# Feed-forward down projections: high halves of the weights by a casting DMA, low halves by an ACT negation and a DMA that adds the weights

## The chip, the core and the metric

One core of one Trainium2 chip runs the whole program once. The metric is device time in microseconds, the median of the timed executions. TensorE (PE in the profile) multiplies, VectorE (DVE), ScalarE (ACT) and GpSimd (POOL) work element by element, SyncE (SP) issues DMAs. Each engine works through its own list of instructions in order and waits at semaphores for the others.

## What is computed

The reference is ten blocks in a row on one activation of 256 tokens by 1024 columns, all in float32. Six of them are the feed-forward block that the change touches:

```python
def swiglu(h, w_gate, w_up, w_down):
    return (jax.nn.silu(h @ w_gate) * (h @ w_up)) @ w_down
```

The inner width is 2816, so gate and up are 1024 x 2816 and down is 2816 x 1024. Each block has an RMS norm ahead of it, some one behind it, and a residual. Between the feed-forward blocks (F1, F3, F4, F6, F8, F10 in the code) stand a convolution with windowed attention ("even"), a forgetting attention ("fox"), an mLSTM ("ml") and a chunked attention with relative positions ("rel"). All weights are read once.

## The kernel before

**Two halves of each weight.** TensorE's fast float32 mode (fp32r) keeps fewer bits than float32. The kernel therefore splits every operand into a high half hi, rounded to fp32r, and a low half lo = w - hi, and makes each product from three matmuls: xh·wh + xh·wl + xl·wh (`mm3`). A matmul has 128 rows and 512 columns.

**Weight stream.** The weights come as 264 units of 1 MB, [128, 2048] each, in the order of use, through `unit` (lines 156 to 178). A DMA of SP loads a unit into one of two `raw` buffers (line 281). For each of the two halves of 1024 columns ACT casts raw to hi (line 207), and DVE forms lo = raw - hi (line 217). hi and lo lie in `hl`, a pool of 20 buffers of [128, 1024], four to a unit. An `hl` buffer is free again when the last matmul that reads it is done, a `raw` buffer when the last subtraction that reads it is done.

**A feed-forward block** (`ffn`) has 11 chunks of 256 inner columns. A chunk has three units: two of gate and up, one of down. For both token blocks b of 128 rows, 24 matmuls per block make gate and up in a PSUM bank (`mm`), ACT and DVE make silu(gate)·up from it, two transposes on PE (line 277) and a split on ACT and DVE give `gt`, and 12 matmuls per block add the chunk's part of the down projection into `acc`. So a chunk has 72 matmuls of 512 columns.

**Order.** Nothing is ordered by hand. The program records all operations with a priority each, and `schedule` plays them against a table of durations, one list per engine, picks buffers as they come free, and emits what results. The table `NUDGE` shifts the priorities of named pieces. The list of an engine is then fixed, and on the chip each instruction only waits for its data and buffers. `load(..., after=...)` adds an order in that plan alone; it makes no wait on the chip.

Of the kernel before, what the change touches and what calls it, by code (L numbers as in the profile page):

```python
# [15 lines left out]
       ("ACT", "PE"): 205.0}  # L16

# [50 lines left out]
class Op:  # L68
    __slots__ = ("eng", "dur", "em", "key", "n", "deps", "succ", "rd", "wr", "end", "start", "vs",
                 "lab", "table", "lat", "avail", "seq", "soft", "ins", "hist")  # L70


class Rec:
    def __init__(self, tc, tags, nudge):
        self.tc, self.nc = tc, tc.nc
        self.tags = tags
        self.ops = []
        self.key = 0.0
        self.grp = None
        self.lab = ""  # L80
        self.phys = {}
        self.nv = 0
        self.meas = None
        self.nudge = nudge
# [67 lines left out]
    def _add(self, o, key):  # L152
        o.key = self.key if key is None else key
        o.n = len(self.ops)
# [89 lines left out]
    def ttr(self, out, a, b, scale, init, op0, op1, accum, key=None):  # L244
        """out = (a op0 b) * scale, accum = its reduction by op1"""
        n = self.n_of(a)
        self.op("DVE", (66 + n) / 0.96 + 8, [a, b], [out, accum],
                lambda: self.nc.vector.tensor_tensor_reduce(  # L248
                    self.res(out), self.res(a), self.res(b), scale, init, op0, op1, self.res(accum)), key=key)
# [15 lines left out]
    def mm(self, out, l, r, start, stop, key=None):  # L265
        n = self.n_of(r)
        if r.v.dt == F32R:
            d = max(107.0 if self.shape(l)[1] > 64 else 53.5, n / 2.4) + 2.5
        else:
            ls = self.shape(l)  # L270
            d = 126.0 if ls[1] == 64 else 2 * max(107.0, n / 1.2) + 4
# [3 lines left out]
    def tr(self, out, in_, ident, key=None):  # L275
        self.op("PE", 109.0, [in_, ident], [out],
                lambda: self.nc.tensor.transpose(self.res(out), self.res(in_), self.res(ident)), key=key)  # L277
# [15 lines left out]
    def schedule(self, sem=130.0):  # L293
# [21 lines left out]
        engs = ["PE", "ACT", "DVE", "DMA"]  # L315
# [4 lines left out]
        table = None  # L320
# [7 lines left out]
        while left:  # L328
# [80 lines left out]
            d = o.dur  # L409
            if o.table is not None and table != o.table:  # L410
# [49 lines left out]
class Net:  # L460
# [40 lines left out]
    def near(self, key):  # L501
        return self.units.get(min(int(key), max(self.units, default=0)))

# [24 lines left out]

    def wsl(self, un, c0, n):
# [5 lines left out]
    def rstd(self, ss, w, n, key, more=False, cut=1):  # L535
        """[P, w] sums of squares (parts of them) -> rsqrt(ss / n + eps), Newton from the exponent trick"""
# [29 lines left out]
    def split_T(self, src, n, hi, lo, key, o0=0, pk=None):  # L566
        """transposes n [128,128] blocks of src into hi + lo at column block o0"""
# [10 lines left out]
    def ssq(self, b, key):  # L578
        """sums of squares of the halves of x"""
# [7 lines left out]
    def gain_T(self, b, g, key):  # L587
        """x * g, transposed and split"""
# [26 lines left out]
    def norm(self, b, g):  # L615
        """(x * g).T in two parts, and per token 1 / rms, half of it, half its square"""
# [9 lines left out]
    def mm3(self, out, x, w, first, last, key):  # L626
        """out += x.T @ w from halves: groups of one k-block"""
# [6 lines left out]
    def proj(self, b, xs, us, u0, n, per, grp=2):  # L634
        """bank [128, n] = x @ W; units hold `per` k-blocks of n columns each"""
# [16 lines left out]
    def oproj(self, b, acc, hi, lo, o0, un, u0, first, last):  # L652
        """acc[2 banks] += o @ W; unit holds 2 k-blocks of 1024 columns"""
# [13 lines left out]
    def postnorm(self, b, acc, g, scale):  # L667
        """x += scale * rmsnorm(acc) * g"""
# [22 lines left out]
    def ffn(self, gi, post, name, exps=lambda b, ch: False):  # L691
# [10 lines left out]
        for ch in range(NCH + 1):  # L702
            if ch < NCH:
                for i in range(3):
                    un[ch * 3 + i] = self.unit(u0 + ch * 3 + i)
# [36 lines left out]
    # the 4 heads of a group lie in the order HM: those on partitions 0-63 first, then those on 64-127  # L742
    def attn_group(self, b, key, qT, kT, v, bias, sgn, O, oc, den, sink=None, nd=2):
        """4 heads of one query block. qT [128, 2 pairs x 128]; kT, v: per pair or key block; sgn * (scores + bias) are negative logits"""
# [62 lines left out]
    def bias_tile(self, b, name, j, key):  # L807
        """additive bias of 4 heads of a query block: for one key block or two"""
# [14 lines left out]
    def k_T(self, b, kT, pt, key):  # L823
        """bank [128, 2 pairs x 128] -> kT [128, 2 pairs x 256]"""
# [4 lines left out]
    def qk_T(self, b, key, bank, rs, kT, sgn=1.0):  # L829
        """row-layout bank [tok, 512] -> (qT [128, nq*128] scaled, kT) via transposes"""  # L830
# [13 lines left out]
    def logsig(self, z, w, out, key):  # L844
        """out = min(z, 0) - log1p(exp(-|z|)), [P, w]"""
# [29 lines left out]
    def gates(self, b, xs, gu, u0, key):  # L875
        """bank [128, 16] = x @ W for 16 columns: W is the stationary side, the sum is turned afterwards"""
# [593 lines left out]
def _cols(w, c0, n):  # L1470
    """[1024, cols] -> units of n-wide columns, 2048 // n k-blocks each: [units, 128, 2048]"""
# [4 lines left out]
def _rows(w):  # L1476
    """[K, 1024] -> units of two k-blocks: [K / 256, 128, 2048]"""
# [11 lines left out]
def arrange(i):  # L1489
# [68 lines left out]
CFG = dict(lead=4, ahead=0, cb=2, fb=6, dd=4, ab=3, vb=2, ncst=784, stages=99, rk=3, bl=3, cg=6, vp=0, du=4, nd=0, k4=2, xb=1, k2=1)  # L1558

NUDGE = {  # L1560
# [17 lines left out]
    "even attn b1": -2, "even attn b1 p": -5, "even conv": -6, "even conv b0 p": 10.5, "even conv b1 p": 14,  # L1578
# [70 lines left out]
```

## Time and profile before

| | |
|---|---|
| median of 3 runs | 1593.97 us (1592.77 to 1594.99) |
| profiled execution, first to last instruction (span) | 1591.4 us |
| PE busy | 1573.6 us (99%) |
| DVE busy | 1015.5 us (64%) |
| ACT busy | 837.4 us (53%) |
| POOL busy | 0.2 us |
| DMA | 296.83 MB, queue of SP busy 50.9% of 16 engines |

The profiled execution lies 2.57 us under the median of the runs: its span counts from the first to the last instruction of the program, and what lies around it is in the timed runs alone. Matmuls are pipelined, and the ends of their rows are modelled, so PE's busy time also holds short waits between two matmuls.

### The profile page before, as it was taken

The numbers are of one execution on the slowest core, as the hardware profiler recorded it, in microseconds if no ns is written. First come the engines' busy times: TensorE is split into PE (matmuls) and PEld (weight loads), VectorE is DVE, ScalarE is ACT, GpSimd is POOL, SyncE is SP. The second block draws the span as 40 slices with busy tenths as digits, with TensorE's granted clock in tenths as the row PEclk, the third lists the DMA queues.
The fourth block names the chain that finished last, engine by engine and source line by source line (L and its number), as shares of the span: only waits on it lengthen the run. The fifth ranks groups of instructions, "written<-read, shape, count | busy, mean of one in ns | idle before, by whom it ended". The sixth has DMA issues, their size and how long they took to land.

```text
span 1591.4 us, 20430 instructions
## 1 busy us (share of the span) xinstructions
PE 1573.6 (99%) x7714; PEld 1289.5 (81%) x7714; DVE 1015.5 (64%) x1969; ACT 837.4 (53%) x1400; POOL 0.2 (0%) x4
## 2 busy tenths in 40 slices
PE   8999999999999999999999999999999999999998
PEld 6888888888888888887788888788888887788886
DVE  6555689854558555677964557887545576755544
ACT  6444556744455454566854445655444457754443
POOL 0000000000000000000000000000000000000000
PEclk9999999999999999999999999999999999999999
DMA  6655585355554555446444554445544645354542
GB/s 244 217 185 211 176 299 184 117 184 188 215 215 151 210 185 211 161 179 208 169 161 183 204 219 160 146 146 198 199 175 169 238 173 202 142 185 185 208 175 80
DMA packets 49587, 296.83 MB, mean 187 GB/s; under 512 B 5408, under 2 KB 8912, under 8 KB 16720
## 3 DMA queue, kind: packets, MB, share of 16 engines
q1 hardware_dynamic: 49488, 295.52, 50.9%
q8 instruction: 60, 0.98, 0.2%
q14 instruction: 39, 0.32, 0.1%
HBM read 294.43 MB, written 1.07 MB: 186 GB/s over the span
## 4 chain that ended last, share of the span: by engine, by line
PE 93%; DVE 3%; DMA 2%; ACT 1%; issue 0%; SPq 0%; ACTq 0%; DVEq 0%
PE mm L273 60%; PE acc L273 28%; PE mm L277 5%; DMA raw<-in_w 2%; DVE hl L217 1%; DVE b L236 1%; ACT hl L207 1%; ACT b L207 1%; DMA x<-in_x 0%; DVE s L236 0%; DVE xt L236 0%; DVE b L248 0%; ACT xt L207 0%; DVE x L236 0%; SPq L281 0%
## 5 line engine op out<-in xcount | busy, mean ns | idle before, releaser
L273 PE MATMUL mm<-hl,xt 128*128 128x512 f32 (+1 forms) x4224 | 1013.0, 393 | 0.6 <-DVE xt L217 0.3
L273 PEld LDWEIGHTS mm<-hl,xt 128*128 128x128 f32 x4224 | 778.0, 188 | 161.4 <-DVE hl L217 2.2
L217 DVE TENSOR_TENSOR hl<-raw,hl 128x1024 fp32r<-128x1024 f32 (+1 forms) x518 | 618.0, 1213 | 350.2 <-ACT hl L207 259.5
L207 ACT ACTIVATE hl<-raw 128x1024 fp32r<-128x1024 f32 (+1 forms) x518 | 522.3, 1048 | 332.6 <-DMA raw<-in_w 168.1
L273 PE MATMUL acc<-hl,gt 128*128 128x512 f32 x1584 | 385.8, 393 | 0.0
L273 PEld LDWEIGHTS acc<-hl,gt 128*128 128x128 f32 x1584 | 293.1, 188 | 59.4 <-ACT gt L207 0.2
L207 ACT ACTIVATE b<-mm,s 128x256 f32<-128x256 f32 (+2 forms) x188 | 94.0, 509 | 219.9 <-PE mm L273 214.7
L236 DVE SCALAR_TENSOR_TENSOR b<-mm,s,b 128x256 f32<-128x256 f32 x132 | 63.3, 481 | 98.4 <-ACT b L207 98.1
L277 PE MATMUL mm<-cst,b 128*128 128x128 f32 (+1 forms) x680 | 109.4, 272 | 3.0 <-DVE s L248 2.5
L277 PEld LDWEIGHTS mm<-cst,b 128*128 128x128 f32 (+1 forms) x680 | 85.4, 140 | 32.2 <-ACT b L207 3.7
L207 ACT ACTIVATE gt<-mm 128x256 fp32r<-128x256 f32 x132 | 50.0, 378 | 92.1 <-PE mm L277 84.6
L273 PE MATMUL acc<-hl,xt 128*128 128x512 f32 x384 | 96.0, 397 | 0.7 <-DVE xt L217 0.7
L217 DVE TENSOR_TENSOR gt<-mm,gt 128x256 fp32r<-128x256 f32 x132 | 55.2, 419 | 51.7 <-ACT gt L207 49.2
L273 PEld LDWEIGHTS acc<-hl,xt 128*128 128x128 f32 x384 | 70.0, 188 | 16.5 <-issue 1.4
L207 ACT ACTIVATE b<-b,s 128x128 f32<-128x128 f32 (+2 forms) x146 | 60.0, 442 | 15.0 <-DVE s L236 7.2
L236 DVE SCALAR_TENSOR_TENSOR s<-s 128x1 f32<-128x1 f32 (+2 forms) x260 | 47.8, 184 | 7.9
L207 ACT ACTIVATE b<-x 128x512 f32<-128x512 f32 x44 | 27.6, 628 | 23.0 <-DVE x L217 11.8
L207 ACT ACTIVATE xt<-mm 128x512 fp32r<-128x512 f32 x44 | 25.4, 595 | 22.0 <-PE mm L277 21.8
L236 DVE SCALAR_TENSOR_TENSOR b<-aT,cst,b 128x256 f32<-128x256 f32 x75 | 31.8, 477 | 0.0
L217 DVE TENSOR_TENSOR xt<-mm,xt 128x512 fp32r<-128x512 f32 x44 | 29.5, 685 | 3.0 <-ACT xt L207 2.4
L207 ACT ACTIVATE b<-mm 128x512 f32<-128x512 f32 (+4 forms) x44 | 21.5, 504 | 13.0 <-PE mm L277 11.2
L273 PE MATMUL mm<-aT,b 128*128 128x128 f32 (+1 forms) x232 | 28.2, 276 | 0.0
(75 smaller groups left out, 454.9 us busy)
## 6 DMA issues: line engine op xcount, KB each, us to landing
raw<-in_w SPq DMA_DIRECT2D x256, 1024.0 KB, 4.8
g<-in_gains SPq DMA_DIRECT2D x18, 512.0 KB, 6.2
b<-in_diag SPq DMA_DIRECT2D x8, 512.0 KB, 5.7
b<-dr SPq DMA_DIRECT2D x12, 256.0 KB, 5.3
g<-in_relb SPq DMA_DIRECT2D x4, 512.0 KB, 5.8
b<-in_diag SPq DMA_DIRECT2D x4, 448.0 KB, 5.3
x<-in_x SPq DMA_DIRECT2D x4, 256.0 KB, 5.3
raw<-in_w SPq DMA_DIRECT2D x4, 256.0 KB, 5.3
```

The source lines that it names most:

```text
L207: return self.nc.scalar.activation(self.res(out), self.res(in_), func, **kw)
L217: lambda: self.nc.vector.tensor_tensor(self.res(out), self.res(a), self.res(b), op), key=key)
L236: lambda: self.nc.vector.scalar_tensor_tensor(self.res(out), self.res(a), self.res(s), self.res(b), op0, op1, **kw), key=key)
L273: lambda: self.nc.tensor.matmul(self.res(out), self.res(l), self.res(r), start=start, stop=stop), key=key)
L277: lambda: self.nc.tensor.transpose(self.res(out), self.res(in_), self.res(ident)), key=key)
```

## The change

The down projection's units (one in three within the feed-forward blocks, 66 of 264) no longer go through `raw`. For each of their 132 halves, GpSimd issues a DMA that reads the float32 weights from memory and writes them into the hi buffer as fp32r, which casts on the way; ACT writes lo = -hi; and a second DMA of GpSimd reads the same weights again and adds them into lo. The other units are loaded and split as before. The cast on ACT is replaced one for one by the negation; 132 subtractions on DVE and 66 loads of 1 MB on SP go; 264 DMAs of 512 KB on GpSimd come in.

```diff
+    def pload(self, out, src, nbytes, key=None, add=False, after=None):
+        kw = dict(accum_op=ALU.add) if add else {}
+        o = self.op("POOL", 1100.0, [src] + [out] * add, [out],
+                    lambda: self.nc.gpsimd.dma_start(out=self.res(out), in_=self.res(src), **kw), lat=2000.0 + nbytes / 220.0, key=key)
+        if after is not None:
+            o.deps.append(after)
...
+    def unit_dma(self, u):
...
+        for c0 in range(0, 2048, 1024):
+            sl = slice(c0, c0 + 1024)
+            hi, lo = r.t("hl", name="hi"), r.t("hl", name="lo")
+            r.pload(hi[:, :], src[:, sl], P * 4096, key=u, after=self.near(u - self.c["pa"]))
+            r.act(lo[:, :], hi[:, :].bitcast(F32), AF.Copy, scale=-1.0, key=u - self.c["ahead"])
+            r.pload(lo[:, :], src[:, sl], P * 4096, key=u, add=True)
...
-                    un[ch * 3 + i] = self.unit(u0 + ch * 3 + i)
+                    un[ch * 3 + i] = self.unit_dma(u0 + ch * 3 + i) if i == 2 else self.unit(u0 + ch * 3 + i)
...
+TURN = {("R", "T"): 27.0, ("T", "R"): 36.0, ("R", "F"): 100.0, ("T", "F"): 60.0}
...
-            d = max(107.0 if self.shape(l)[1] > 64 else 53.5, n / 2.4) + 2.5
+            d = n / 2.4 + (13.3 if ls[1] > 64 else 7.0)
...
-    "F1 D10 b0 p": -1.75, "F1 D10 b1 p": -6.25, "F1 D3 b1 p": 0.25, "F1 D4 b0 p": -3, "F1 D4 b1 p": -2.25, "F1 D6 b0 p": -4.5,
+    "F1 D0 b0 p": 14, "F1 D0 b1 p": -14, "F1 D1 b0 p": 11.5, "F1 D1 b1 p": -1, "F1 D10 b0 p": -14, "F1 D10 b1": -0.25,
...
-    r.keep = dict(b4=cfg["k4"], b2=cfg["k2"])
+    r.keep = dict(hl=4, b4=cfg["k4"], b2=cfg["k2"])
```

The planner's durations for PE are new (a cost for a change between fp32r matmuls, transposes and plain float32 matmuls among them), `keep` holds back four `hl` buffers for earlier units, and all of `NUDGE` is replaced by a longer table. So the order on every engine is new; which matmuls there are, and how many, is not. Three places follow, as the two programs have them. Names are buffers: hl_81 to hl_100 are the 20 weight buffers, cst the constants, x_63 and x_64 the two token blocks.

At the program's start, SP's list before:

```order
L281 DMA cst_68<-in_cst 128x136
L281 DMA x_63<-in_x 128x512
L281 DMA raw_76<-in_w 128x512
L281 DMA x_63<-in_x 128x512
L281 DMA raw_76<-in_w 128x512 x3
L281 DMA x_64<-in_x 128x512 x2
L281 DMA raw_77<-in_w 128x2048
```

SP's list there now:

```order
L293 DMA cst_68<-in_cst 128x136
L293 DMA x_63<-in_x 128x512 x2
L293 DMA x_64<-in_x 128x512 x2
L293 DMA raw_76<-in_w 128x512 x4
L293 DMA raw_77<-in_w 128x2048
```

All four loads of activations now stand ahead of the first weights. GpSimd's list there, with the semaphores that each row waits for (before, it issued nothing):

```order
L308 DMA hl_81<-in_w 128x1024
L308 DMA hl_83<-in_w 128x1024
L308 DMA hl_90<-in_w 128x1024 [waits Activation_49]
L308 DMA hl_92<-in_w 128x1024 [waits Activation_49]
L308 DMA hl_93<-in_w 128x1024
L308 DMA hl_95<-in_w 128x1024
```

The first two rows, 512 KB each, wait for nothing, so they start beside SP's first loads.

Within the feed-forward block F3, GpSimd's list now. hl_86 and hl_84 are hi and lo of one half of a down unit; DMASW is a semaphore of GpSimd's own earlier DMAs:

```order
L308 DMA hl_86<-in_w 128x1024 [waits DMASW2_49,DVE_49,PE_49]
L308 DMA hl_98<-in_w 128x1024 [waits DMASW3_49]
L308 DMA hl_97<-in_w 128x1024 [waits DMASW4_49,PE_49]
L308 DMA hl_84<-in_w 128x1024 [waits DMASW5_49,Activation_49]
L308 DMA hl_83<-in_w 128x1024 [waits DMASW6_49,Activation_49]
L308 DMA hl_81<-in_w 128x1024 [waits DMASW7_49,PE_49]
L308 DMA hl_94<-in_w 128x1024 [waits DMASW0_49,DVE_49,PE_49]
```

The casting DMA into hl_86 waits until PE has done with what lay there, the adding DMA into hl_84 waits for ACT's negation, and two casting DMAs of other halves stand between them, one of which waits for PE too. ACT's list there now:

```order
L213 ACTIVATE hl_88<-raw_76 128x1024
L213 ACTIVATE hl_84<-hl_86 128x1024
L213 ACTIVATE hl_83<-hl_98 128x1024
L213 ACTIVATE b_161<-mm_193,s_182 128x256
L213 ACTIVATE hl_85<-raw_76 128x1024
```

Two negations stand in ACT's list between casts of other units; what follows them on ACT waits until they have their data.

In the stage "even", PE's list before, around the softmax of one group of heads (mm<-b,b are its scores, mm<-cst,b the transposes of its result, mm<-aT,b the convolution, acc<-hl,xt the output projection):

```order
L273 MATMUL mm_195<-b_161,b_154 128x256
L273 MATMUL acc_186<-b_146,b_160 64x128 x4
L273 MATMUL mm_193<-aT_129,b_138 128x128 x8
L277 MATMUL mm_194<-cst_68,b_136 128x128 x4
L273 MATMUL mm_193<-aT_129,b_137 128x128 x7
L277 MATMUL mm_195<-cst_68,b_136 128x128 x4
```

PE's list there now, cut out of a run of 24 matmuls of the output projection, of which the last three are shown:

```order
L284 MATMUL acc_186<-hl_97,xt_107 128x512
L284 MATMUL acc_186<-hl_82,xt_107 128x512
L284 MATMUL acc_186<-hl_97,xt_104 128x512
L289 MATMUL mm_194<-cst_68,b_136 128x128 x4
L289 MATMUL mm_196<-cst_68,b_136 128x128 x4
L284 MATMUL mm_193<-aT_129,b_137 128x128 x8
```

The 24 matmuls now stand between the scores and the transposes, where eight small matmuls of the convolution and four of the previous group stood.

## Rows read from the trace of the kernel before

**Rows 1.** The page: span, busy time of PE, granted clock.

```profile
span 1591.4 us, 20430 instructions
...
PE 1573.6 (99%) x7714; PEld 1289.5 (81%) x7714; DVE 1015.5 (64%) x1969; ACT 837.4 (53%) x1400; POOL 0.2 (0%) x4
...
PEclk9999999999999999999999999999999999999999
```

**Rows 2.** Busy time by stretch: start, F1, even, the end; columns in the first row.

```profile
core 0: us, PE busy (x) PEld busy (x) DVE busy (x) ACT busy (x) POOL busy (x), PEclk, DMA share, GB/s
0.00:25.00 25.00, 19.20 (x78) 14.91 (x79) 16.94 (x58) 17.52 (x39) 0.20 (x4) 1.00 0.68 244
25.00:240.00 215.00, 214.46 (x1026) 178.03 (x1025) 136.04 (x214) 105.19 (x154) 0.00 (x0) 1.00 0.61 220
240.00:310.00 70.00, 66.44 (x432) 55.92 (x431) 64.12 (x179) 50.11 (x120) 0.00 (x0) 1.00 0.41 149
...
1460.00:1592.00 132.00, 123.69 (x559) 101.37 (x557) 65.98 (x96) 53.70 (x78) 0.00 (x0) 0.98 0.42 155
```

**Rows 3.** Who PE waited for: total us, times, longest us.

```profile
PE mm L277 <- DMA x<-in_x: 5.8, 2, 3.9
PE mm L277 <- DVE s L248: 2.5, 1, 2.5
PE acc L273 <- DVE xt L217: 0.7, 1, 0.7
PE mm L277 <- ACT b L207: 0.4, 1, 0.4
PE mm L273 <- DVE xt L217: 0.3, 1, 0.3
PE mm L277 <- DVE b L236: 0.2, 1, 0.2
```

**Rows 4.** Waits of DVE and ACT ahead of the split of weights.

```profile
DVE hl L217 <- ACT hl L207: 259.5, 146, 8.5
...
ACT hl L207 <- PE mm L273: 143.6, 97, 8.9
```

**Rows 5.** Groups by form: count, busy us, mean ns, idle before and releasers.

```profile
L273 PE MATMUL mm<-hl,xt 128*128 128x512 f32 x4176 | 1007.3, 394 | 0.6 <-DVE xt L217 0.3
...
L217 DVE TENSOR_TENSOR hl<-raw,hl 128x1024 fp32r<-128x1024 f32 x512 | 614.8, 1221 | 350.0 <-ACT hl L207 259.3 <-PE mm L273 73.1 <-PE acc L273 12.8
L207 ACT ACTIVATE hl<-raw 128x1024 fp32r<-128x1024 f32 x512 | 519.4, 1054 | 332.3 <-DMA raw<-in_w 167.9 <-PE mm L273 143.4 <-PE acc L273 17.7
```

**Rows 6.** Loads of raw within F1: issue ns min/median/max, landing us min/median/max.

```profile
L281 SPq DMA_DIRECT2D raw<-in_w x39: 327/328/336, 26.6 to 232.2; - x39
...
DMA to landing us min/median/max: 4.7/4.8/6.8
```

**Rows 7.** The first 14 us: issues of SP, loads' landing (raw alone), PE.

```profile
4.96 0.76 SPq L281 DMA_DIRECT2D raw<-in_w  x1
...
DMA to landing us min/median/max: 3.7/5.7/8.2
...
7.64 3.10 PE L273 MATMUL mm<-hl,xt 128*128 128x512 f32 x6
...
13.48 8.05 PE L273 MATMUL mm<-hl,xt 128*128 128x512 f32 x33
```

**Rows 8.** PE in the stage even, us and duration, idle time before.

```profile
258.11 2.05 PE L273 MATMUL mm<-aT,b 128*128 128x128 f32 x16
262.61 0.63 PE L277 MATMUL mm<-cst,b 128*128 128x128 f32 x4 [2.45 <-DVE s L248]
```

**Rows 9.** PE's last rows.

```profile
1575.12 2.89 PE L273 MATMUL acc<-hl,gt 128*128 128x512 f32 x12
1577.85 0.38 PE L277 MATMUL mm<-cst,b 128*128 128x128 f32 x2
1577.98 5.71 PE L273 MATMUL acc<-hl,gt 128*128 128x512 f32 x24
```

More of the change, by code (lines that the diff above doesn't have):

```diff
@@ L69 @@
     __slots__ = ("eng", "dur", "em", "key", "n", "deps", "succ", "rd", "wr", "end", "start", "vs",
-                 "lab", "table", "lat", "avail", "seq", "soft", "ins", "hist")
+                 "lab", "table", "lat", "avail", "seq", "soft", "ins", "hist", "kind")
 class Rec:
@@ L79, in __init__ @@
         self.grp = None
+        self.kind = None
         self.lab = ""
@@ L153, in _add @@
         o.key = self.key if key is None else key
+        o.kind = self.kind
         o.n = len(self.ops)
@@ L266, in mm @@
         n = self.n_of(r)
+        ls = self.shape(l)
         if r.v.dt == F32R:
-            d = max(107.0 if self.shape(l)[1] > 64 else 53.5, n / 2.4) + 2.5
-        else:
-            ls = self.shape(l)
-            d = 126.0 if ls[1] == 64 else 2 * max(107.0, n / 1.2) + 4
+            d = n / 2.4 + (13.3 if ls[1] > 64 else 7.0)
+        elif ls[1] == 64:
+            d = 155.0
+        elif ls[0] == 64:
+            d = 117.0 + 0.766 * n
+        else:
+            d = 2 * max(112.0, n / 1.2)
+        self.kind = "R" if r.v.dt == F32R else "F"
         self.op("PE", d, [l, r], [out],
@@ L275, in tr @@
     def tr(self, out, in_, ident, key=None):
+        self.kind = "T"
         self.op("PE", 109.0, [in_, ident], [out],
@@ L290, in store @@
                 lambda: self.nc.sync.dma_start(self.res(dst), self.res(in_)), lat=2000.0, key=key)
+    def pload(self, out, src, nbytes, key=None, add=False, after=None):
[4 more added lines that the diff above has]
+            o.deps.append(after)
+            after.succ.append(o)
+            o.soft = after
+        return o
     def schedule(self, sem=130.0):
@@ L314, in schedule @@
                 v.slot = None
-        engs = ["PE", "ACT", "DVE", "DMA"]
+        engs = ["PE", "ACT", "DVE", "DMA", "POOL"]
         tfree = dict.fromkeys(engs, 0.0)
@@ L319, in schedule @@
         rdy = {e: [] for e in engs}
-        table = None
+        table = kind = None
         order = []
@@ L409, in schedule @@
             d = o.dur
+            if e == "PE":
+                d += TURN.get((kind, o.kind), 0.0)
+                kind = o.kind
             if o.table is not None and table != o.table:
@@ L501, in near @@
     def near(self, key):
-        return self.units.get(min(int(key), max(self.units, default=0)))
+        return self.units.get(max((u for u in self.units if u <= key), default=-1))
     def unit(self, u, cols=2048, src=None):
@@ L524, in unit @@
                 r.tt(lo[:, sl], s, hi[:, sl].bitcast(F32), ALU.subtract, key=k)
+            his.append(hi)
+            los.append(lo)
+        return his, los
+    def unit_dma(self, u):
+        r = self.r
+        r.lab = f"unit{u}"
+        src = self.a["w"][self.wunit]
+        self.wunit += 1
+        his, los = [], []
+        for c0 in range(0, 2048, 1024):
[4 more added lines that the diff above has]
+            r.pload(lo[:, :], src[:, sl], P * 4096, key=u, add=True)
             his.append(hi)
@@ L1557 @@
     acc=(F32, 512, 4, 1), mm=(F32, 512, 4, 1))
-CFG = dict(lead=4, ahead=0, cb=2, fb=6, dd=4, ab=3, vb=2, ncst=784, stages=99, rk=3, bl=3, cg=6, vp=0, du=4, nd=0, k4=2, xb=1, k2=1)
+CFG = dict(lead=4, ahead=0, cb=2, fb=6, dd=4, ab=3, vb=2, ncst=784, stages=99, rk=3, bl=3, cg=6, vp=0, du=4, pa=2, nd=0, k4=2, xb=1, k2=1)
 NUDGE = {
[17 rows of a table removed]
-    "even attn b1": -2, "even attn b1 p": -5, "even conv": -6, "even conv b0 p": 10.5, "even conv b1 p": 14,
[22 rows of a table removed]
[64 rows of a table added]
+    "even attn b1": 0.75, "even attn b1 p": 7.75, "even conv": 4.5, "even conv b0 p": 14, "even conv b1 p": 5.25,
[60 rows of a table added]
 }
```

161 rows, old and new, of the table NUDGE are left out of this document.

## The prediction

> **What bounds the kernel now.** I read the page first, then busy time by stretch, then the waits of PE, and only then the groups.
>
> The page [rows 1] says that PE is busy 1573.6 us of a span of 1591.4, with a granted clock of 9 tenths or more in all 40 slices, the upper of its two levels (2.4 GHz). Busy time alone would prove little, since it holds short waits between matmuls, so the second look is where the other 17.8 us lie [rows 2]: 5.8 in the first 25 us (25.00 less 19.20), 8.3 in the end (132.00 less 123.69), 3.6 in the stage even (70.00 less 66.44), and 0.5 in the 215 us of F1. The feed-forward stages, which the change edits, have next to no idle PE. The third look names what PE waited for [rows 3]: 9.9 us in all, 5.8 of them the very first loads. For DVE it waited 3.7 us in the whole kernel (2.5 + 0.7 + 0.3 + 0.2), for ACT 0.4, for a DMA of weights never.
>
> The other engines wait for PE, not the reverse. ACT's casts of weights stood 143.6 us until PE had given back a buffer, and DVE's subtractions 259.5 us until ACT had cast [rows 4]. Both are behind a full buffer pool. The pace of PE is 0.24 us a matmul (1007.3 us over 4176) [rows 5].
>
> So the edit takes work from an engine that nobody waits for. What can be won is the few us of PE's waits; what can be lost is larger, since the weights get a longer way.
>
> **The change part by part.** All sums are made against the profiled execution, 1591.4 us; 2.57 us are added at the end to stand beside the runs' median of 1593.97.
>
> 1. *132 subtractions leave DVE*, 1.221 us each [rows 5], 161 us of 1015.5. PE's waits for DVE are 3.7 us and nearly all lie in the stage even, outside the edited units. Taken at 0. The work that hides it is PE's own; it would count only if DVE were the last to come, and in F1 it is busy 136.04 of 215 us.
>
> 2. *132 casts on ACT become 132 negations* of the same size. The nearest row is the cast, 1.054 us [rows 5]; input and output are alike in shape and memory. Difference 0. But the negation now waits for a landing that GpSimd asked for, and what stands behind it in ACT's list (casts, silu, `gt`) waits with it. ACT is busy 105.19 of 215 us in F1 [rows 2], so a late landing of 1 or 2 us is made good before PE sees it; I charge it under 5.
>
> 3. *66 loads leave SP, 264 DMAs come to GpSimd's list*, whose engine was idle. SP's issue took 0.33 us [rows 6]; GpSimd's issue is in no row. Bytes moved in a chunk rise from 3 MB to 4 (two plain units, and one unit read twice): at F1's DMA share of 0.61 [rows 2] that makes about 0.81 if the new kinds move like the old, and over 1 for a while if they move at half the speed. The engines are not full on average, but transfers will meet.
>
> 4. *The start.* Before, 3.2 MB of first loads were down by 13.2 us (the last issued at 4.96, landing 8.2 later) [rows 7], and PE ran without a break from 13.48. The new program puts 1 MB of GpSimd's in the same time, not needed until PE's 73rd weight matmul, and asks for activations ahead of weights. From the first landing at about 2.6 us, 3.2 MB in 10.6 us is 0.30 MB/us, so 1 MB more costs 3.5 us if all of it gets in ahead. It costs nothing if GpSimd comes late or the engines serve SP first, and the new order of SP's loads may even save up to 1 us of PE's 1.9 us wait for the second activation. I take +1.5, the middle, with -1 and +3.5 as ends.
>
> 5. *The new way of a down unit's weights.* A half passes: the hi buffer is given back by PE; the casting DMA lands; ACT negates; the adding DMA lands; PE may read lo. Casting and adding DMAs are in no row. The nearest rows are 1 MB loads of SP: 4.8 us from issue to landing as a rule, 6.8 at worst in F1 [rows 6], and 8.2 in the crowd of the start [rows 7]. The new ones are half as large, but add or cast, and share the engines with SP's stream. So the way is at least 4.8 + 1.05 + 4.8 = 10.7 us and at most, with one cast of ACT in front, 8.2 + 1.05 + 1.05 + 8.2 = 18.5. I take the row of a transfer that has met another, 6.8, twice, with 1.05 for the negation and half a cast in front: 15.2.
>  What it may take is read from the order: I counted, for each of the 132 halves, the matmuls on PE's list from the last that reads the old contents of hi to the first that reads the new lo. The shortest count is 58 (hl_86 and hl_84 in F3, shown above), then 59, 60, 63, 63; 14 halves lie at 70 or below, 24 at 77 or below; the median is 118. At 0.24 us each, 58 matmuls are 13.9 us. A way of 10.7 makes no half late. One of 15.2 makes five late, by 3.3 us together. One of 17.4 makes 17 late, by 27 us together, some 21 if two halves of one unit that are late together count once. One of 18.5 makes 24 late, 50 us or, counted so, 34. I take +3.4, with 0 and +34 as ends.
>  The Trainium skill (DMA: Bandwidth & Descriptors, "Anatomy of one DMA — SWDGE (gpsimd) path") gives a DMA that GpSimd issues about 2.0 us plus its bytes at 436 GB/s; for 512 KB that is an estimate of 3.2 us, a way of 7.5 us, no late half and a sum 3.4 us lower. No row here shows such a DMA, and the formula is for plain copies.
>
> 6. *The new order.* In the stage even PE waited 2.45 us for transposes behind a softmax [rows 8]. Now 24 matmuls of the output projection, 5.8 us at 0.24, stand between the scores and these transposes, so that wait should go: -2.5, with 0 as the other end, since DVE's chain there (busy 64.12 of 70 us [rows 2]) may end late at another place. Returns from transposes to weight matmuls fall from 216 to 164 by the order. Two transposes and the next matmul cost little beyond their work: from 1575.12 to 1577.98 are 2.86 us for 12 matmuls (2.88 at 0.24) with the transposes in it [rows 9]. So 52 fewer are worth at most 1 us; I take -0.5. The end of the list (last 12 matmuls, residual, norm, store) is as before, and its 8.3 us stay.
>
> Sum: 1591.4 - 2.5 - 0.5 + 1.5 + 3.4 = 1593.3 us of span, and with 2.57 around it **1595.9 us**. A measurement of this kernel can tell about 0.2%, 3.2 us, from no change: that is 1590.8 to 1597.2, and the forecast lies inside it. The case as a whole reaches from 1591 to 1597.
>
> **The rivals.**
>
> *Weights in time, start free (faster).* The new DMAs are as quick as SP's, so no half is late, and the start gains what its order promises: 1591.4 - 2.5 - 0.5 - 1 = 1587.4, or 1590.0 measured. It cannot go far: all of PE's waits together are 9.9 us [rows 3], so 1581.5 of span, 1584 measured, is the floor. For it speaks that the shortest lead, 13.9 us, is above two plain landings and a negation. Against it speaks the higher load of the DMA engines. Chance 0.24.
>
> *Late weights in the feed-forward stages (slower).* Casting or adding is slower than copying, or GpSimd's list holds an adding DMA behind a casting one that waits for PE, as it stands before hl_84. It decides from a way of about 15.8 us, where more than five halves are late. At 17.4 us the sum is 1591.4 - 1.5 + 21 = 1610.9, 1613.5 measured; at 18.5 it is 1626. For it speak 24 halves with little room and an order that was planned to the limit of 20 buffers; against it, that 118 matmuls, 28 us, is the median. Chance 0.27.
>
> *DVE holds GpSimd up (slower).* If an issue of GpSimd has to wait for a running subtraction of 1.22 us [rows 5], twice in each way, 15.2 becomes 17.6: about 24 us more than none late, 1591.4 - 1.5 + 24 = 1613.9, 1616.5 measured. Before, GpSimd did nothing, so no row speaks for or against. Chance 0.05. The Trainium skill (SBUF — State Buffer, "Who interferes with whom") says that GpSimd and DVE share a port pair under an exclusive lock, that copies and tensor-scalar work between SBUF operands can keep GpSimd from writing descriptors, and that a tensor-tensor with two SBUF inputs stands against GpSimd's reads alone. By that rule the subtractions cost nothing here; no run here shows it yet.
>
> *The whole crowd at the start, nothing won in even (slower).* 1591.4 + 3.5 + 3.4 - 0.5 = 1597.8, 1600.4 measured. Chance 0.04.
>
> **How the numbers follow.** Forecast 0.40 (within 0.2%), faster 0.24, slower 0.27 + 0.05 + 0.04 = 0.36. The range of 8 in 10 runs from 1586, inside the first rival, to 1618, which takes in the second up to a way of about 17.5 us and leaves out its worst.
>
> **What the profile will show.** The landing of the two kinds of DMA of GpSimd: 6.8 us or less bears out step 5, 8 or more the second rival. PE's waits in the 25 to 240 us: if they stay near 0.5 us, no half is late; if rows of the accumulators name GpSimd's DMA, they are. The wait at about 260 us gone, the first unbroken run of weight matmuls later or earlier than 13.48. DVE's busy time near 855 us with the span hardly moved would show that step 1 is right. The forecast is wrong if the issue on GpSimd takes several us, since two issues are in each way and 264 in one list.

## The result and the profile after

The changed kernel takes **1730.6 us** (median; 1727.3 to 1735.1), the kernel before 1593.4 in the same runs: a ratio of **1.086 [1.085, 1.088]**, 137 us slower. The forecast was 1595.9 with a range of 1586 to 1618.

The page of the changed kernel: span, busy time, granted clock, and the DMA queues (packets, MB, share of 16 engines' span; q1 is SP's, q0 GpSimd's).

```profile
span 1728.2 us, 20746 instructions
...
PE 1623.7 (94%) x7714; PEld 1311.3 (76%) x7714; DVE 869.2 (50%) x1837; ACT 842.3 (49%) x1400; POOL 188.6 (11%) x268
...
PEclk9999999999989999999999998999999999999999
...
q1 hardware_dynamic: 39984, 226.31, 35.8%
q0 software_dynamic: 38016, 138.43, 34.4%
```

Against [rows 1], DVE lost 146 us of work and PE gained nothing from it. PE, with as many matmuls, is busy 50 us longer and idle for 104.5 us instead of 17.8. The second reading is where, by stretch (columns as in [rows 2]):

```profile
core 0: us, PE busy (x) PEld busy (x) DVE busy (x) ACT busy (x) POOL busy (x), PEclk, DMA share, GB/s
0.00:25.00 25.00, 16.05 (x55) 11.93 (x56) 14.29 (x54) 16.57 (x37) 4.31 (x10) 1.00 0.79 266
25.00:240.00 215.00, 195.85 (x856) 158.22 (x855) 89.24 (x139) 93.39 (x133) 27.43 (x38) 0.96 0.78 226
```

In these 215 us, all of them F1 before, there was 0.5 us of idle PE; now there are 19.2, and 856 matmuls are done where 1026 were. The granted clock falls to 0.96. The third reading is what PE waited for (us, times, longest), beside [rows 3]:

```profile
PE acc L284 <- DMA hl<-in_w: 37.6, 20, 4.7
PE mm L289 <- DVE b L242: 15.8, 7, 5.4
PE mm L284 <- ACT hl L213: 10.9, 7, 3.0
PE mm L289 <- DMA x<-in_x: 8.0, 3, 4.1
PE acc L284 <- ACT gt L213: 7.3, 3, 6.0
PE mm L284 <- DVE hl L223: 6.3, 10, 0.8
```

The first row is new: PE waits for a DMA of GpSimd, by the order of the lists an adding one all 20 times. PE's waits for ACT and DVE, smaller rows included, sum to 50.2 us, where they were 4.1 [rows 3]. ACT itself stood still too: its negations waited for casting DMAs (page, group of the negation: count, busy, mean ns, idle before it and what ended it), and the DMAs themselves, casting and adding in one row (issue ns, then landing us, min/median/max):

```profile
L213 ACT ACTIVATE hl<-hl 128x1024 fp32r<-128x1024 f32 x132 | 139.3, 1059 | 236.7 <-DMA hl<-in_w 194.7
```

```profile
L308 POOL DMA_DIRECT2D hl<-in_w x264: 530/864/1197, 1.2 to 1703.0; - x132
...
DMA to landing us min/median/max: 3.8/7.3/18.4
```

I paired the DMAs with the negations by their order in the lists. From the issue of the casting DMA to the landing of the adding one, the 132 halves took 17.8 us in the median; one tenth stayed below 13.6, one tenth above 24.0. In means: casting landing 7.3, ACT late by 3.2, negation 1.06, GpSimd late by 0.3, adding landing 8.1. The medians of the two landings are 6.8 (casting) and 7.7 (adding).

One late half, in the timeline of the changed kernel (start, duration, engine, work; in brackets the idle time before and what ended it):

```profile
580.78 1.06 ACT L213 ACTIVATE hl<-hl 128x1024 fp32r<-128x1024 f32 x1 [0.31 <-DMA hl<-in_w]
...
582.14 1.44 POOL L308 DMA_DIRECT2D hl<-in_w  x2 [2.09 <-ACT hl L213]
582.37 0.48 ACT L213 ACTIVATE b<-mm,s 128x256 f32<-128x256 f32 x1
...
582.53 4.61 PE L284 MATMUL acc<-hl,gt 128*128 128x512 f32 x19
...
586.78 1.06 ACT L213 ACTIVATE hl<-hl 128x1024 fp32r<-128x1024 f32 x1 [3.94 <-DMA hl<-in_w]
588.14 0.88 POOL L308 DMA_DIRECT2D hl<-in_w  x1 [4.56 <-ACT hl L213]
...
591.84 0.79 PE L284 MATMUL acc<-hl,gt 128*128 128x512 f32 x1 [4.71 <-DMA hl<-in_w]
```

The late half is the one that ACT negates at 580.78: its casting DMA had taken 10.1 us to land. The first of the two DMAs that GpSimd issues at 582.14 is its adding one. That one lands 9.7 us later, at 591.80; PE has run dry at 587.14 and waits 4.71 us for it. The whole way of this half took 21.2 us. The 3.94 us that ACT stands in the same time, and the DMA issued at 588.14, belong to the next down unit: ACT's list is held up for work that PE does not need yet. What follows is seen in the granted clock of the same place:

```profile
584.00:588.00 4.00, 3.13 (x14) 2.25 (x12) 0.00 (x0) 1.06 (x1) 0.00 (x0) 1.00 1.03 303
588.00:592.00 4.00, 0.16 (x1) 0.16 (x1) 0.00 (x0) 0.00 (x0) 0.88 (x1) 0.64 1.08 302
592.00:596.00 4.00, 4.00 (x13) 3.31 (x14) 0.77 (x2) 2.17 (x4) 0.87 (x1) 0.51 0.66 135
596.00:600.00 4.00, 4.00 (x19) 3.27 (x18) 0.50 (x2) 1.42 (x3) 0.00 (x0) 1.00 0.88 131
```

After a gap of 4.7 us PE runs 4 us at 0.51, the lower level (1.2 GHz), and does 13 matmuls, six of them narrow transposes, where the next 4 us have 19. So the gap is paid for again, here with about 2 us. The clock records of this trace show 15 such stretches in the course of the kernel, each behind a gap of 1.9 to 6.0 us in PE's work. They hold 67.4 us of PE's busy time; at half the speed that is a loss of 33.7 us.

### The profile page after: what moved, and what is told of

It is laid out like the page before. It is cut to its first block, busy times and chain, and to the rows that moved or that the text cites. A ratio compares the mean times of both kernels' runs of the same rounds, so it can differ in the third digit from the quotient of the medians.

```text
span 1728.2 us, 20746 instructions
## 1 busy us (share of the span) xinstructions
PE 1623.7 (94%) x7714; PEld 1311.3 (76%) x7714; DVE 869.2 (50%) x1837; ACT 842.3 (49%) x1400; POOL 188.6 (11%) x268
## 3 DMA queue, kind: packets, MB, share of 16 engines
q0 software_dynamic: 38016, 138.43, 34.4%
## 5 line engine op out<-in xcount | busy, mean ns | idle before, releaser
L284 PE MATMUL mm<-hl,xt 128*128 128x512 f32 (+1 forms) x4224 | 1019.2, 396 | 22.5 <-ACT hl L213 10.9
L284 PEld LDWEIGHTS mm<-hl,xt 128*128 128x128 f32 x4224 | 788.4, 190 | 196.2 <-ACT hl L213 14.6
L223 DVE TENSOR_TENSOR hl<-raw,hl 128x1024 fp32r<-128x1024 f32 (+2 forms) x386 | 461.2, 1212 | 411.6 <-ACT hl L213 266.9
L213 ACT ACTIVATE hl<-raw 128x1024 fp32r<-128x1024 f32 (+2 forms) x386 | 392.3, 1046 | 213.0 <-DMA raw<-in_w 88.5
L284 PE MATMUL acc<-hl,gt 128*128 128x512 f32 x1584 | 410.8, 409 | 45.0 <-DMA hl<-in_w 37.6
L284 PEld LDWEIGHTS acc<-hl,gt 128*128 128x128 f32 x1584 | 305.2, 197 | 120.6 <-DMA hl<-in_w 48.7
L308 POOL DMA_DIRECT2D hl<-in_w x264 | 188.4, 758 | 1515.0 <-ACT hl L213 503.5
L213 ACT ACTIVATE hl<-hl 128x1024 fp32r<-128x1024 f32 x132 | 139.3, 1059 | 236.7 <-DMA hl<-in_w 194.7
L223 DVE TENSOR_TENSOR gt<-mm,gt 128x256 fp32r<-128x256 f32 x132 | 54.3, 421 | 148.9 <-ACT gt L213 129.8
L289 PE MATMUL mm<-cst,b 128*128 128x128 f32 (+1 forms) x680 | 107.1, 277 | 20.6 <-DVE b L242 15.8
L289 PEld LDWEIGHTS mm<-cst,b 128*128 128x128 f32 (+1 forms) x680 | 81.9, 142 | 51.4 <-DVE b L242 20.0
L242 DVE SCALAR_TENSOR_TENSOR s<-s 128x1 f32<-128x1 f32 (+3 forms) x260 | 47.7, 184 | 8.0
L213 ACT ACTIVATE b<-x 128x512 f32<-128x512 f32 x44 | 27.7, 630 | 28.3 <-DVE x L223 17.5
L223 DVE TENSOR_TENSOR xt<-mm,xt 128x512 fp32r<-128x512 f32 x44 | 29.1, 684 | 4.0 <-ACT xt L213 3.9
```

The costliest lines, as they stand in the source:

```text
L213: return self.nc.scalar.activation(self.res(out), self.res(in_), func, **kw)
L223: lambda: self.nc.vector.tensor_tensor(self.res(out), self.res(a), self.res(b), op), key=key)
L242: lambda: self.nc.vector.scalar_tensor_tensor(self.res(out), self.res(a), self.res(s), self.res(b), op0, op1, **kw), key=key)
L284: lambda: self.nc.tensor.matmul(self.res(out), self.res(l), self.res(r), start=start, stop=stop), key=key)
L308: lambda: self.nc.gpsimd.dma_start(out=self.res(out), in_=self.res(src), **kw), lat=2000.0 + nbytes / 220.0, key=key)
```

## The experiments

The theory after the result: the way of a half is longer than its lead, and what is late is paid for by PE directly, through the lists of ACT and DVE, and through the clock. Rivals: the new order itself; the load on the DMA engines whatever the way; ACT's stop alone.

### The new order without the new DMAs

**order_only.** In `ffn`, all units by `self.unit`:

```diff
-self.unit_dma(u0 + ch * 3 + i) if i == 2 else self.unit(u0 + ch * 3 + i)
+self.unit(u0 + ch * 3 + i)
```

> The changed kernel with its new order and planner, but the down projections' weights loaded and split in the old way (one 1 MB load of SP, casts on ACT, subtractions on DVE). The first theory, that the loss comes from the weights' new way and not from the new order, expects 1588 to 1600 us, as before the change. The rival, that the new order itself costs (more switches at the wrong places, fewer free buffers), expects 1650 us or more, most of the 137 us.

1651.3 us, ratio 1.037 [1.035, 1.039]. By its number that is the rival's bound (1650 us or more), though at 58 us it is not most of the 137. But the run does not test the changed kernel's order: with other work the planner makes another order, and the table of priorities (`NUDGE`) is then one for a program that it was not made for. PE's longest waits in this run are for DVE ("PE mm L289 <- DVE b L223", 16.8 us), not for weights. So I kept the order and changed only what its steps emit.

**order_held.** The planner sees the changed kernel; GpSimd copies a constant in the place of each casting DMA, the adding one is not emitted (the edits of this and the following runs are shown shortened).

```diff
 r.pload(hi[:, :], src[:, sl], ...)
+r.ops[-1].em = [lambda: gpsimd.tensor_copy(hi, cst[:, 0:1].to_broadcast([P, 1024]))]
 ...
 r.pload(lo[:, :], src[:, sl], ..., add=True)
+r.ops[-1].em = []
```

> The changed kernel, same order, with no DMA of GpSimd at all: a copy of a constant on GpSimd stands in the place of each casting DMA, ACT negates it, the adding DMA is left out, and so are the weights of the down projections. What is left is the new order with weights that are always in time. If the 20 us that remain without adding DMAs belong to the order: 1608 to 1616 us. If they belong to the casting DMAs: 1590 to 1598 us.

1607.5 us, 1.009 [1.006, 1.012], at the lower edge of the order's range: with weights in time the new order costs **14 us**.

```profile
span 1605.1 us, 20422 instructions
...
PE 1578.6 (98%) x7714; PEld 1292.7 (81%) x7714; DVE 887.0 (55%) x1837; ACT 841.1 (52%) x1400; POOL 154.0 (10%) x136
```

PE is idle for 26.5 us. The 14 us are not quite pure: the run has no transfers of down weights at all, and DVE is busy 887.0 us, where it was 869.2 in the changed kernel. In the stage even the wait for DVE's `s` is gone as forecast, but another of the same size stands there (waits of PE from 240 to 330 us):

```profile
PE mm L289 <- DVE b L223: 2.0, 1, 2.0
PE mm L289 <- ACT b L213: 0.5, 2, 0.3
```

### The transfers by themselves

**bench.** No computation; chains of 512 KB transfers, each after the landing of the one before, at the end beside a stream of SP's 1 MB loads.

> The computation is left out; only transfers of 512 KB are timed, each after the landing of the one before: plain ones of SP, plain, casting and adding ones of GpSimd, a casting and an adding one at once, and both beside a stream of SP's 1 MB loads. If casting and adding are slow in themselves, they land alone in 5 us or more where a plain one takes 4 or less, and company adds little. If they are slow only in company, they land alone in 4 us or less and in 7 us or more beside the stream.

The issues (KB each, median us to landing; `sp` and `gp` are SP's and GpSimd's, `pr` a casting and an adding one at once, `bg` beside the stream):

```profile
bgcast<-in_w POOLq DMA_DIRECT2D x6, 512.0 KB, 6.0
bgadd<-in_w POOLq DMA_DIRECT2D x6, 512.0 KB, 9.6
spcopy<-in_w SPq DMA_DIRECT2D x4, 512.0 KB, 3.7
gpcopy<-in_w POOLq DMA_DIRECT2D x4, 512.0 KB, 4.1
gpcast<-in_w POOLq DMA_DIRECT2D x4, 512.0 KB, 4.1
gpadd<-in_w POOLq DMA_DIRECT2D x4, 512.0 KB, 5.5
...
prcast<-in_w POOLq DMA_DIRECT2D x4, 512.0 KB, 5.0
pradd<-in_w POOLq DMA_DIRECT2D x4, 512.0 KB, 6.9
```

Casting costs nothing over a plain copy of GpSimd. Adding costs 1.4 us more than casting alone and 3.6 more in company. So the expectation holds in neither form: the kind matters, and so does the company.

### The same order, one property of the way at a time

Six runs keep the changed order and change what is emitted. All leave out a part of the split of the down weights, as each expectation says.

**no_add**: the adding DMA is not emitted.

> The changed kernel, same order of all that is left, without its 132 adding DMAs: the low halves stay the negated high halves, so the sums of the weights' low parts are left out. If the second landing is what makes halves late (a way of 17.8 us in the median falls to 8.5), PE's waits go: 1590 to 1605 us. If ACT, which stands still until a casting DMA has landed and holds silu and its later work back, is the cause, the loss shrinks only as far as the casting DMAs land earlier: 1630 to 1700 us.

**no_neg**: no negation, the second DMA casts, so that the two landings lie side by side.

```diff
-gpsimd.dma_start(out=lo, in_=src, accum_op=ALU.add)
+gpsimd.dma_start(out=lo, in_=src)
-scalar.activation(lo, hi, AF.Copy, scale=-1.0)
```

> The changed kernel, same order, with the negations left out and the adding DMAs made casting ones of the same bytes, so that the subtraction of the high halves is left out: nothing on ACT waits for a DMA of GpSimd, and the two landings of a half lie side by side, but the DMA engines move the same bytes. If the serial way or ACT's list is the cause: 1590 to 1605 us. If the load on the DMA engines alone is the cause: 1680 us or more, with landings of 7 us and above.

**serial_cast**: the negation stays, the second DMA casts.

> The changed kernel, same order, with the adding DMAs made casting ones that overwrite the negation, so that the subtraction of the high halves is left out: a half still passes landing, negation, landing, and ACT still waits for the first, but no DMA adds. If the one-after-the-other way and ACT's stop behind a landing are the cause: 1670 us or more. If the adding kind is the cause (9.6 us of landing against 6.0 of a casting one beside a stream of loads): 1615 to 1640 us, as in the runs without an adding DMA.

**par_add**: the second DMA adds, but ACT fills `lo` from a constant instead of from `hi`.

> The changed kernel, same order, but ACT fills the low buffer from a constant instead of negating the high half, so that the subtraction is left out: the adding DMAs are there, ACT waits for no landing and the two landings of a half lie side by side. If the adding kind alone is the cause (it holds the DMA engines longest): 1680 us or more. If the one-after-the-other way with ACT's stop is the cause: 1615 to 1640 us.

**add_half**: as the changed kernel, `lo[:, 0:512]` alone is added to.

> The changed kernel, same order, in which the adding DMAs move only the first 512 of 1024 columns, so that half of the weights' addition is left out: 256 KB each, as many DMAs, the same chain. If an adding DMA costs by its bytes (it keeps the DMA engines busy), about half of the 115 us between the runs with and without it goes: 1660 to 1680 us. If it costs by being one more landing in the chain, whatever its size: 1700 us or more.

**act_stop**: as no_neg, with ACT negating `hi` in place.

> As the run without negations and adding DMAs (both DMAs of a half casting, side by side, the subtraction of the high halves left out; 1620 us), but ACT negates the high half in place, so ACT waits for a landing at the same place as in the changed kernel while the low half is already on its way. If ACT's stop behind a landing (with silu and gt queued behind it) is what the one-after-the-other way costs: 1645 to 1660 us, as with two casting DMAs one after the other (1654). If the length of the way is: 1612 to 1628 us.

| run | way of a half | us | over before | PE busy | PE idle | q0, share of 16 engines |
|---|---|---|---|---|---|---|
| order_held | no DMA | 1607.5 | 14 | 1578.6 | 26.5 | 0 |
| no_add | cast, negate | 1615.6 | 22 | 1579.9 | 34.2 | 13.8% |
| no_neg | cast beside cast | 1619.8 | 26 | 1580.6 | 33.3 | 26.7% |
| act_stop | the same, ACT waits for a landing | 1635.6 | 43 | 1588.8 | 44.5 | 26.6% |
| serial_cast | cast, negate, cast | 1654.3 | 61 | 1596.0 | 54.7 | 26.8% |
| add_half | cast, negate, add 256 KB | 1656.5 | 63 | 1594.7 | 58.8 | 26.3% |
| par_add | cast beside add | 1681.0 | 88 | 1609.5 | 76.2 | 34.7% |
| changed kernel | cast, negate, add | 1730.6 | 137 | 1623.7 | 104.5 | 34.4% |

(Ratios with intervals: no_add 1.014 [1.012, 1.016], no_neg 1.016 [1.013, 1.020], act_stop 1.027 [1.024, 1.030], serial_cast 1.038 [1.035, 1.041], add_half 1.039 [1.036, 1.042], par_add 1.055 [1.045, 1.065]; two runs each, so a step between two rows is known to some 5 us, from par_add to some 15.)

Most of these runs came out between the two ranges of their expectations: no_add and no_neg nearer the lower one, serial_cast and act_stop in the middle. add_half lies just under its range for a cost by bytes (1660 to 1680). Only par_add met a range, barely (1680 or more; its two runs took 1674.4 and 1687.5). So no single cause carries the loss.

Read downwards, without no_add and add_half: the order 14 us, casting DMAs side by side another 12, ACT's stop 17, the longer way 18, the adding kind 76. The shares depend on the path. The adding kind beside a casting DMA costs 62 (par_add less no_neg); one landing after the other costs 35 with a casting DMA (serial_cast less no_neg) and 50 with an adding one (changed kernel less par_add). ACT's stop has no fixed price either: in no_add ACT stands 72.8 us behind casting DMAs, and the run loses 8 us to order_held. And no_neg frees ACT of 132 negations (busy 714.9 us instead of 842.3), so that part of the 17 us may be this work.

no_neg moves the same bytes as the changed kernel, and its queue's landings are 7.0 us in the median against 7.3; it loses 26 us, not 137. So bytes and slow landings alone do not do it. PE's waits for a weight DMA show the kind: 1.8 us in no_neg, and

```profile
PE acc L284 <- DMA hl<-in_w: 7.6, 5, 2.4
```

in serial_cast, but

```profile
PE acc L284 <- DMA hl<-in_w: 38.1, 22, 4.9
```

in par_add, where ACT waits for no landing of GpSimd at all. In act_stop both expectations missed; of the 35 us between no_neg and serial_cast about half go with ACT's stop and half with the longer way.

What makes the adding kind dear is how long it keeps the DMA engines. In no_neg, 26.7% of 1613.9 us carry 138.43 MB: 321 GB/s. In the changed kernel 34.4% of 1728.2 are 594 us; taking 69.2 MB of casting ones at no_add's 13.8% of 1614.1, 223 us, the adding half took 372 us, 186 GB/s: an estimate of 1.7 times as long for the same bytes and packets. Half the columns (add_half) bring q0 back to 26.3%, by the same sum 212 us for the adding half, and the time to that of serial_cast: it costs mostly by its bytes. The Trainium skill (Collectives: The Full Stack, "The bandwidth ceiling: the fold count and why AG ≠ RS ≠ AR") says of another operation that an add in the DMA path needs two source reads on one ring and halves the rate. The 1.7 here points the same way; no run here shows the reads. SP's own stream is slowed beside the adding kind too: in the 25 to 240 us its 1 MB loads land in 6.2 us in the median in the changed kernel and 6.8 in par_add, where it was 4.8 before and 5.0 in no_neg. No run separates what PE lost by these late loads from what it lost by ACT's stop.

**neg_pool**: the changed kernel with the negation on GpSimd.

```diff
-scalar.activation(lo, hi, AF.Copy, scale=-1.0)
+gpsimd.tensor_scalar(lo, hi, -1.0, None, ALU.mult)
```

> The changed kernel, same order and same result, with the negations on GpSimd in place of ACT: the way of a half stays as long, or gets a little longer, but ACT no longer waits for landings. If ACT's stops (194.7 us behind landings of casting DMAs, with silu and the copies of gt queued behind them) carry the larger part of the loss: 1665 us or less. If late halves alone do: 1715 us or more.

1796.6 us, 1.128 [1.124, 1.131]. ACT no longer waits for landings, and it is 66 us worse. The group of the negation on GpSimd:

```profile
L567 POOL TENSOR_SCALAR hl<-hl 128x1024 fp32r<-128x1024 f32 x132 | 397.1, 3013 | 433.4 <-DMA hl<-in_w 293.7 <-PE mm L284 114.1 <-PE acc L284 17.2
```

It takes 3.0 us instead of 1.06, and GpSimd now stands for 293.7 us behind landings, with the next casting DMAs queued behind it. The stop was moved into the list that starts the transfers. So the run does not clear ACT's stop, and it cannot say what the way's length alone costs: a slower negation and the stop of GpSimd's list came together. Together they are dearer than ACT's stop.

### More and less lead

**lat8**: the planner takes 8.0 us for a landing. **old_numbers**: the priorities of the kernel before. **half**: the new way in the odd chunks alone. The edit of lat8:

```diff
-lat=2000.0 + nbytes / 220.0
+lat=2000.0 + nbytes / 87.0
```

> The changed kernel, same work and result, its order made anew by a planner that takes 8.0 us for a landing of GpSimd's DMA instead of 4.4. Counted from the order as in the prediction, 1 half has 74 matmuls or fewer (17.8 us) from the release of its hi buffer to the first use of its lo, where the changed kernel has 22. If leads that are shorter than the way are what the loss comes from, most of it goes: 1645 us or less. If ACT's stops behind landings or the load on the DMA engines are, whatever the lead: 1690 us or more.

> The changed kernel with the table of priorities of the kernel before, same work and result; 35 halves have 74 matmuls or fewer, against 22, and the sum of what they lack to a way of 17.5 us is 53 us against 28. If leads decide: 1800 us or more. If the load on the DMA engines decides, which is the same: 1715 to 1745 us.

> The changed kernel with the new way for the down units of the odd chunks alone (60 halves), the others split in the old way; the planner orders it anew. 10 halves have 74 matmuls or fewer, against 22. If the loss follows the halves on the new way one for one: 1593 + 14 for the order + half of 123 = 1668 us. If it comes from transfers that meet (adding DMAs of neighbouring chunks beside the stream): 1640 us or less.

1713.3, 1783.2 and 1704.7 us (1.075 [1.070, 1.080], 1.119 [1.110, 1.128], 1.070 [1.066, 1.073]). Since each is an order made anew, each was also run without GpSimd's DMAs, as in order_held:

> The order planned for a landing of 8.0 us (1713 us with the DMAs), with no DMA of GpSimd: a copy of a constant stands for the casting DMA, the adding DMA and the weights of the down projections are left out. It gives this order's own cost. If longer leads do help, and were hidden by a worse order: 1640 us or more, so that the DMAs cost 75 us or less here where they cost 123 in the changed kernel. If leads do not help: 1600 to 1615 us, the DMAs' cost being 100 us or more.

> The order with the table of priorities of the kernel before (1783 us with the DMAs; 35 halves with little lead against 22), with no DMA of GpSimd, in the same way. If the lack of lead decides what the DMAs cost: 1620 us or less, so that they cost 160 us or more. If it does not: 1655 to 1665 us, the DMAs' cost being the 123 us of the changed kernel.

> The order of the run with the new way in the odd chunks alone (1705 us), with no DMA of GpSimd, the down weights of the odd chunks left out. If the DMAs' cost follows the number of halves on the new way (60 of 132): about 1649 us, 56 us less, and the order made anew costs the rest. If the loss there is the DMAs' too: 1625 us or less.

A half's lead is the number of matmuls on PE's list between the release of its hi buffer and the first use of its lo, at 0.24 us each; "lacking" is what the leads fall short of a way of 17.5 us, summed over all halves. The direct waits are PE's row `acc<-hl,gt <- DMA hl<-in_w`.

| order | halves with 74 matmuls of lead or fewer | lacking to 17.5 us, sum | direct waits | with DMAs | without | DMAs' cost |
|---|---|---|---|---|---|---|
| lat8 | 1 | 0.7 us | 22.4 | 1713.3 | 1663.4 | 50 |
| half (60 halves) | 10 | 10.6 us | 10.9 | 1704.7 | 1669.1 | 36 |
| changed kernel | 22 | 28.5 us | 37.6 | 1730.6 | 1607.5 | 123 |
| numbers of before | 35 | 52.7 us | 59.4 | 1783.2 | 1650.1 | 133 |

By their times alone lat8 came out on the side of "leads do not decide" (1690 or more), old_numbers between its ranges and half above both. The runs without DMAs correct that for lat8: its order costs 71 us by itself, and 1663.4 is on the side of leads that help. More lead takes the DMAs' cost from 123 to 50 us, so the lead matters, as the first theory has it. But less lead adds only 10 us, where 37 or more were expected, and half, with 45% of the halves, costs 36 and not 56. PE's direct waits do follow the lead, except in lat8; the cost behind them does not. And the orders made anew cost 58 to 77 us of their own (1650.1 to 1669.1 against about 1592): none of the three is better than the kernel before. In lat8 the way grows to 21.2 us in the median, which may be why 22.4 us of direct waits remain.

## Why the prediction was wrong, point by point

- **What bounds the kernel** was right: PE. DVE's relief (step 1) showed no gain, as forecast; its busy time fell to 869 us, near the 855 named.
- **Step 2 failed**: "a late landing of 1 or 2 us is made good before PE sees it". It was charged under 5 us, and the sum has no term for it. ACT stood 194.7 us behind casting DMAs, 63 times, the longest 15.1 us, and silu and `gt` stood with it. act_stop measures about 17 us for that stop with a short way.
- **Step 3** held in its bytes and in F1's DMA share (0.78, estimated 0.81), but by halves that differ: casting DMAs move like plain ones, adding ones at some 186 GB/s. "If the new kinds move like the old" was true of one of the two.
- **Step 4**: in the first 25 us PE was busy 16.05 us instead of 19.20, so the start lost 3.2, near the upper end of 3.5. With the order alone it is 18.96.
- **Step 5 is the term that was mis-sized: +3.4 stood for about 119 us** (137 less the 14 of the order and 4 of the start). The way was taken as 15.2 and bounded by 18.5; its median was 17.8, and a tenth lay above 24.0. The typical landing was close to the 6.8 taken (6.8 casting, 7.7 adding, so between the two signs on record, 6.8 and 8); the longest took 18.4 us, where the worst row of before had 8.2, and ACT came 3.2 us late in the mean, where half a cast was taken. Yet the price was wrong far more than the way. Of what the step priced, PE's direct waits for late halves, the trace has 37.6 us, about the upper end of 34. The rest was not in the sum at all.
- **Step 6 failed**: -3 was taken, +14 measured (order_held). The wait in even was replaced by another, and PE's busy time rose by 5.0 us where 0.5 were to be won; two stretches at the lower clock took 3.3 of the 5.0.
- **No term for the clock.** [rows 1] show 9 tenths in every slice, and the sum assumed it would stay so. The same matmuls in the same order take 1578.6 us of PE in order_held and 1623.7 in the changed kernel; over the whole span the granted clock is 0.997 there and 0.976 here. By the clock records the lower level cost PE 3.3 us there and 33.7 here, so it makes 30 of these 45 us.

The 137 us by what PE did: 14 the order (order_held less before); then, between the two traces of the same order, 30 the lower clock, 15 more of busy time at the full clock, 38 direct waits for a weight DMA, 36 waits for DVE and ACT, which were late themselves (all their rows sum to 50.2 us, in order_held to 14.1), and 4 at the start (8.0 less 4.3 for `x`). That is 137. Busy time also holds short waits, so the 15 us may be such; no run separates them. That ACT's stop and SP's slowed loads made DVE and ACT late is argued from their lists; act_stop gives the size for the first alone.

The second rival named the mechanism and its place, and its condition (a way of 15.8 us or more) was met; its prices, 1613.5 for a way of 17.4 and 1626 for 18.5, missed by over 100 us for the same reason as step 5: lateness was added up half by half as if nothing stood behind it. Of its two reasons the first holds, adding being slower than copying; the second does not, since GpSimd's list held an adding DMA up by 0.3 us in the mean. The rows offered nothing for an adding DMA but loads of another kind. The rival of DVE holding up GpSimd is not seen: an adding issue takes 0.87 us (mean) with DVE idle in bench and 0.87 (median of the 132, by the pairing) here. By the rule of the Trainium skill (SBUF — State Buffer, "Who interferes with whom") work with two SBUF inputs, as the subtractions are, keeps GpSimd from reads alone and should not hold its issues; the trace agrees. By the Trainium skill's formula for GpSimd's DMAs (DMA: Bandwidth & Descriptors, "Anatomy of one DMA — SWDGE (gpsimd) path"), 3.2 us was the estimate, the page naming no kind of transfer for it; alone they took 4.1 and, adding, 5.5. The measurement decides.

## What to carry to other kernels

When a step moves from an engine to a DMA, ask first which in-order list will stand behind its landing, and price a late piece with everything queued there and with the clock after the gap; here the direct waits were 38 us of 137. Compare leads with the spread of the way, not with its typical value, and measure a kind of transfer that the trace doesn't show, alone and in company, before its time is taken from another kind. A table of priorities belongs to one program: rebuild the order around other work and its own loss (58 us and more here) hides what you wanted to see, so hold the order and change what it emits.

## What the hardware showed unexpectedly

- A casting DMA of 512 KB is as fast as a plain one of GpSimd (4.1 us both, 3.7 by SP). An adding one takes 5.5 us alone and 9.6 beside a stream of loads, and by the estimate above keeps the DMA engines 1.7 times as long.
- GpSimd's issue of a casting DMA takes 0.53 us, with DVE idle (bench) and with DVE busy 54% of the time (no_neg); that of an adding one takes 0.87, in bench and in the changed kernel.
- Behind gaps of 1.9 to 6.0 us in PE's work the granted clock fell to the lower level, 15 times in the changed kernel; behind the one of 4.7 us PE ran 4 us at 0.51.
- A negation of 128x1024 takes 1.06 us on ACT and 3.0 on GpSimd.
